# Where a product's two operands begin in SBUF: other strips between the pools of a decoder trunk

## The chip, the cores and the metric

The kernel runs on one core of one Trainium2 chip. The metric is the device time of one execution in microseconds (us); lower is better. One core's SBUF has 128 partitions, and "where a tile begins" means the byte of each partition at which it begins.

## The reference

The reference is a decoder trunk of two layers on 512 tokens of width 1024, in fp32. Each layer applies four blocks to x, and after each one adds the result to a scaled x and normalises:

```python
x = layer_norm(a * x + 0.5 * swiglu_ffn(x, w_in[i, 0], w_out[i, 0]))
x = layer_norm(a * x + h)      # layer 0: diff_attention(x); layer 1: pool_mixer(x)
x = layer_norm(a * x + memory_cross_attention(x, mem, wq[i], wkv[i], wo[i]))
x = layer_norm(a * x + 0.5 * swiglu_ffn(x, w_in[i, 1], w_out[i, 1]))
```

`swiglu_ffn` is `(silu(x @ w_gate) * (x @ w_up)) @ w_out` with an inner width of 2816. `diff_attention` has 8 heads with a rotary position code and the difference of two softmaxes. `pool_mixer` takes causal means over windows of 2, 4, 8 and 16 tokens and a small product for each group of columns. The cross attention has 4 heads and 256 memory tokens.

## The kernel before

Stages follow one another: for each layer `ffn_first` (L1362), `mixer` (L1377), `cross_attention` (L1288), `ffn_second` (L1373). Each opens two groups of tile pools: `stage_pools` (L163) holds the weights, raw from the DMA (`ra`, `rc`, `raw`) and split (`wh`, `wl`); `phase_pool` (L149) holds the activations. Pools are laid out one after the other in the order in which they are opened, so that an unused strip between two of them (`pad`, L134) moves the begin of all tiles behind it. `to_x` opens a strip of 448 bytes, `to_w` one of 64 (the constants `APART` = 64, `ROUND` = 512).

**Products.** An fp32 operand is split into a high part and a rest (`split`: ScalarE copies the high part at L114, VectorE subtracts at L115). `mm3` (L193) makes a product of three matmuls, high by high, high by rest and rest by high:

```python
mm(out, w[0], x[0], ...)    # L197: stationary w, moving x
mm(out, w[0], x[1], ...)    # L198
mm(out, w[1], x[0], ...)    # L199
```

The operand named first in the profile (`x<-xh,wh`) is the moving one, streamed through TensorE; the second is the stationary one, 128 x 128, loaded into the array by a weight load (PEld) that runs beside the matmul ahead of it. Moving operands have 512 or 256 columns.

**FFN.** `up` (L560) makes seven block products of 256 columns (`x`, `y`, `z`, moving `xh`, `xl` or `xe`, stationary `wh`, `wl`), which are combined into the four blocks of a Strassen-like scheme. `down` (L675) does the same on the way back, with 512 columns: `px`, `py`, `pz`, moving `wh`, `wl`, stationary `ha`, `hb`. The two alternate: mostly a down-product of 12 matmuls, then 48 matmuls of up-products, and so on. The last three blocks of a stage go through `plain_down` (L762), `ps` with 512 columns and stationary `xe`, whose moving operands are `wh`, `wl` for the first half and `hb`, `ha` for others.

**The other stages.** The differential attention has `q` and `k` (512 columns), `v` (256), scores, and `po<-v,a`. The cross attention has `pk`, `pv` (keys and values of the memory, 256 columns), `xq` (512, and 256 in part of layer 1), `xs` (scores, 256) and `xo` (512). `to_tokens` (L437) projects back to the tokens: `ps` with 512 columns, moving `wh`, `wl` and other tiles in which weights were split, stationary `oT`. The pool mixer has band products and `pooled`.

**Order.** `weave` (L202) interleaves a main stream of products with a side stream by counted costs; on each engine the instructions stand in program order. DMAs of weights are issued from SP's queue (L574, L225) and, with an addition, from GpSimd's (L578). A tile in a pool that takes over bytes of an earlier pool waits for the last reader of these bytes; so the order of pools also decides which loads wait for what.

**The start of the pool mixer** (layer 1). While its first products run, `load_memory` (L1156) transposes the memory tokens and splits them into `mem0h`, `mem0l` and on (L1175, L114, L115), the keys `pk` of two heads are made early, and `pool_weights` (L1061) loads `pw` (L1066), `ps` (L1073, the scale; L1074, the bias) and multiplies them on VectorE.

Of the kernel before, what the change touches and what calls it, by code (L numbers as in the profile page):

```python
# [9 lines left out]
F32 = mybir.dt.float32  # L10
# [7 lines left out]
P = 128  # L18
# [33 lines left out]
APART, ROUND, LINE = 64, 512, 480  # L52
# [52 lines left out]
class Trunk:  # L105
# [31 lines left out]
            pool = ctx.enter_context(self.pool("pad"))  # L137
            pool.tile([P, nbytes // 4], F32, tag="pad", name="pad")

    def to_x(self, ctx):  # L140

        self.pad(ctx, ROUND - APART)

    def to_w(self, ctx):

        self.pad(ctx, APART)

    @contextmanager
    def phase_pool(self, gain, spare, **bufs):  # L149

        self.gain, self.spare, self.bufs, self.phase = gain, spare, bufs, {}
        with ExitStack() as ctx:
            for t in bufs:
                if t == "_x":
                    self.to_x(ctx)
                else:
                    self.phase[t] = ctx.enter_context(self.pool(t))
            yield  # L160

    @contextmanager
    def stage_pools(self, w, raw, order):  # L163

        with ExitStack() as ctx:
            self.stage = {}
            for n in order:
                if n == "wl" and order[0] == "mem" or n == "wh" == order[0]:
                    self.to_w(ctx)
                self.stage[n] = ctx.enter_context(self.pool(n))  # L170
            self.banks = {n: ctx.enter_context(self.pool(n, space=PSUM)) for n in ("px", "py", "yz")}
            self.w_bufs, self.raw_bufs, self.aux_turn = w, raw, 0
            yield
# [982 lines left out]
    def load_memory(self, tag=None):  # L1156

        nc = self.nc
        src = self.a["mem"][0].rearrange("(m p) (h d) -> p m h d", p=P, h=2)
        if tag:  # L1160
            raw = [[self.tmp(tag) for h in range(2)] for m in range(2)]
            for m in range(2):
                for h in range(2):
                    nc.sync.dma_start(raw[m][h], src[:, m, h])
        else:
            t = self.raw_tile((2, 2, S))
            nc.sync.dma_start(t, src)
            raw = [[t[:, m, h] for h in range(2)] for m in range(2)]
        self.memT = []
        for c in range(0, KC, 2):  # L1170
            pt = self.aux("pt").rearrange("p (c m n) -> p c m n", c=2, m=2)
            for i in range(2):
                for m in range(2):
                    o = (c + i) % 4 * P
                    self.nc.tensor.transpose(pt[:, i, m], raw[m][c // 4][:, o : o + P], self.ident)  # L1175
            t = tuple(self.stage["mem"].tile([P, 2, MEM], F32R, name=f"mem{c}{n}") for n in "hl")
            self.split(t[0], t[1], pt.rearrange("p c m n -> p c (m n)"))
            self.memT += [(t[0][:, i], t[1][:, i]) for i in range(2)]
        if tag and LINE < 480:
            self.stage["mem"].tile([P, (480 - LINE) // 4], F32, name="mempad")  # L1180

    def xa_kv(self, w, h):
        nc = self.nc
# [102 lines left out]
            yield from self.xa_head(*self.heads[h][1])  # L1286

    def cross_attention(self, layer, ln):  # L1288
        bufs = dict(q=8, oT=10, gb=2)
        if layer == 0:  # L1290
            self.kv = []
            mem = self.side_pool("mem")
            with self.other_pools():
                self.stage["mem"] = mem
                with self.phase_pool(("gb", "gb"), "p", pT=6, p=4, kv=8, _x=0, **bufs):
                    self.kvp = self.phase["kv"]
                    with self.tc.high_priority():
                        self.load_memory("p")
                    self.xa(layer, ln)
            self.close_side()  # L1300
        else:
            with self.later, self.phase_pool(("gb", "gb"), "p", _x=0, pT=6, p=4, **bufs):
                self.xa(layer, ln)

    def xa(self, layer, ln):
# [44 lines left out]
        self.side.pop().__exit__(None, None, None)  # L1350

    def ffn_pools(self):
        return self.stage_pools(4, dict(ra=4, rc=3), ("wh", "wl", "ra", "rc"))

    def other_pools(self, order=("wh", "wl", "raw")):
        return self.stage_pools(5, dict(raw=2), order)

    def ffn_phase(self, **more):
        bufs = dict(b1=1, b3=1, b2=1, b4=1, _x=0, xe=6, hb=4, sp=4, ha=4, sr=1, hr=3)
        return self.phase_pool(("hr", "sr"), "sp", **bufs, **more)  # L1360

    def ffn_first(self, layer, ln):  # L1362
# [13 lines left out]

    def mixer(self, layer, ln):  # L1377
        if layer == 0:
            bufs = dict(low=4, rt=2, a=4, p=4, o=1, qk=8, _x=0, v=4, oT=11)
            with self.other_pools(), self.phase_pool(("v", "v"), "rt", **bufs):  # L1380
                self.diff_attention(layer, ln)
            self.close_side()
        else:
            self.later = ExitStack()
            self.later.enter_context(self.other_pools(("mem", "wl", "raw", "wh")))
            self.kvp = self.later.enter_context(self.pool("kv"))
            bufs = dict(pw=1, pb=2, ps=2, ones=1, _x=0, pooled=20, sq=1)
            with self.phase_pool(("pooled", "pooled"), "sq", **bufs):
                side = self.pool_mixer(layer, ln)
                with self.tc.high_priority():  # L1390
                    self.load_memory()
                next(side)
                self.kv = []
                self.weave(self.early_kv(layer, 2), side, 900, 4300)
            self.close_side()
# [45 lines left out]
```

## Time and profile before

| | |
|---|---|
| time, median of 3 runs | 1972.75 us (1970.02 to 1975.78) |
| the profiled execution | 1976.36 us |
| its span in the trace | 1974.6 us |
| granted TensorE clock | 0.995 |
| DMA | 277.96 MB, mean 141 GB/s |
| GpSimd busy | 320.1 us (16%) |

The span is the time from the first to the last recorded instruction of the profiled execution. Rows of the timeline give the start in us, the length in us, the engine, the line of the kernel, the operation, and out<-in; a bracket at the end gives the idle time before and what ended it. The length of a matmul in the profile holds the depth of the pipeline: consecutive matmuls overlap, and how fast they follow is read from the starts.

### The profile page before, as it was taken

How to read it: one execution, taken by the hardware profiler on the slowest of the kernel's cores; microseconds unless marked ns; L12 is line 12 of the kernel's file. 1: busy time of each engine (PE TensorE's matmuls, PEld its weight loads, DVE VectorE, ACT ScalarE, POOL GpSimd, SP SyncE). 2: the span in 40 equal slices, each digit the busy share in tenths (PEclk: the TensorE clock that was granted, in tenths of full speed). 3: DMA queues.
4: the chain of work that ended last, by engine and by line, in shares of the span. 5: the costliest groups of instructions: out<-in, count | busy, mean ns of one | idle time of the engine just before them, and what ended most of it. 6: DMA issues, size and time to landing. Idle time of an engine off the chain costs nothing. (4 is left out here: it accounts for less than half of the span.)

```text
span 1974.6 us, 32506 instructions
## 1 busy us (share of the span) xinstructions
PE 1920.2 (97%) x13104; PEld 1749.0 (89%) x13104; DVE 1566.1 (79%) x2208; ACT 1016.0 (51%) x1545; POOL 320.1 (16%) x297
## 2 busy tenths in 40 slices
PE   7999999999999999999999999999999999999998
PEld 7999998888778888999998999999788889899996
DVE  7888987888867558789887888888777457888886
ACT  5554553466655435555553655555445435555552
POOL 1122121111211002221220311211100013111211
PEclk9999999999999999999999999999989999999999
DMA  9988772322134316977783787877254336877861
GB/s 238 197 171 181 166 156 64 89 65 86 45 116 139 108 65 160 203 176 166 145 193 112 149 176 168 181 171 139 77 171 131 104 96 143 168 173 170 184 143 46
DMA packets 246743, 277.96 MB, mean 141 GB/s; under 512 B 8256, under 2 KB 212544, under 8 KB 246592
## 3 DMA queue, kind: packets, MB, share of 16 engines
q0 software_dynamic: 92928, 92.29, 30.3%
q1 hardware_dynamic: 153664, 183.59, 28.8%
q8 instruction: 103, 1.69, 0.3%
q14 instruction: 48, 0.39, 0.1%
HBM read 273.75 MB, written 2.10 MB: 140 GB/s over the span
## 5 line engine op out<-in xcount | busy, mean ns | idle before, releaser
L578 POOL DMA_DIRECT2D ra<-in_ffn_w_in_dram x132 | 171.4, 1316 | 1017.0 <-DVE wl L115 850.9
L114 ACT CAST wh<-ra 128x1024 fp32r<-128x1024 f32 x184 | 192.9, 1053 | 218.1 <-DMA ra<-in_ffn_w_in_dram 55.7
L115 DVE TENSOR_TENSOR wl<-ra,wh 128x1024 fp32r<-128x1024 f32 x184 | 223.6, 1221 | 82.1 <-ACT wh L114 81.4
L114 ACT CAST wh<-rc 128x1024 fp32r<-128x1024 f32 x136 | 142.7, 1053 | 129.3 <-PE x L198 39.2
L197 PE MATMUL x<-xh,wh 128*128 128x256 f32 x704 | 197.5, 281 | 6.3 <-DVE hr L644 4.1
L197 PE MATMUL x<-xe,wh 128*128 128x256 f32 x704 | 195.3, 277 | 3.1 <-ACT sp L639 1.7
L198 PE MATMUL x<-xl,wh 128*128 128x256 f32 x704 | 196.5, 279 | 1.5 <-DVE xl L115 1.5
L199 PE MATMUL x<-xh,wl 128*128 128x256 f32 x704 | 196.1, 279 | 0.8 <-DVE wl L115 0.8
L198 PE MATMUL x<-xe,wh 128*128 128x256 f32 x704 | 194.8, 277 | 0.0
L199 PE MATMUL x<-xe,wl 128*128 128x256 f32 x704 | 194.7, 277 | 0.0
L115 DVE TENSOR_TENSOR wl<-rc,wh 128x1024 fp32r<-128x1024 f32 x136 | 164.6, 1220 | 27.5 <-ACT wh L114 27.1
L114 ACT CAST wh<-b 128x1024 fp32r<-128x1024 f32 x112 | 117.7, 1051 | 125.7 <-PE x L198 62.0
L115 DVE TENSOR_TENSOR wl<-b,wh 128x1024 fp32r<-128x1024 f32 x112 | 136.8, 1222 | 41.0 <-ACT wh L114 41.0
L197 PEld LDWEIGHTS x<-xh,wh 128*128 128x128 f32 x704 | 133.2, 189 | 9.4 <-issue 4.4
L197 PEld LDWEIGHTS x<-xe,wh 128*128 128x128 f32 x704 | 132.2, 188 | 5.0 <-ACT ha L639 1.9
L198 PEld LDWEIGHTS x<-xl,wh 128*128 128x128 f32 x704 | 133.4, 189 | 3.3 <-DVE xl L115 2.1
L199 PEld LDWEIGHTS x<-xh,wl 128*128 128x128 f32 x704 | 133.2, 189 | 1.0 <-DVE wl L115 1.0
L198 PEld LDWEIGHTS x<-xe,wh 128*128 128x128 f32 x704 | 132.3, 188 | 1.3
L199 PEld LDWEIGHTS x<-xe,wl 128*128 128x128 f32 x704 | 132.4, 188 | 0.0
L115 DVE TENSOR_TENSOR wl<-raw,wh 128x1024 fp32r<-128x1024 f32 x64 | 80.5, 1264 | 56.1 <-ACT wh L114 55.4
L114 ACT CAST wh<-raw 128x1024 fp32r<-128x1024 f32 x64 | 66.6, 1051 | 71.5 <-PE xq L198 22.7
L199 PE MATMUL z<-xh,wl 128*128 128x256 f32 x352 | 97.9, 280 | 4.0 <-DVE wl L115 4.0
(413 smaller groups left out, 6156.5 us busy)
## 6 DMA issues: line engine op xcount, KB each, us to landing
ra<-in_ffn_w_in_dram POOLq DMA_DIRECT2D x132, 512.0 KB, 7.2
rc<-in_ffn_w_in_dram SPq DMA_DIRECT2D x88, 512.0 KB, 6.0
b<-in_ffn_w_out_dram SPq DMA_DIRECT2D x76, 512.0 KB, 5.7
ra<-in_ffn_w_in_dram SPq DMA_DIRECT2D x44, 512.0 KB, 4.7
rc<-in_ffn_w_in_dram POOLq DMA_DIRECT2D x44, 512.0 KB, 9.8
raw<-in_xa_wkv_dram SPq DMA_DIRECT2D x16, 1024.0 KB, 5.3
raw<-in_da_w_qkv_dram SPq DMA_DIRECT2D x16, 512.0 KB, 5.2
raw<-in_xa_wq_dram SPq DMA_DIRECT2D x8, 1024.0 KB, 5.1
```

Of the source, the lines that this page charges most:

```text
L114: self.nc.scalar.copy(hi, src),
L115: self.nc.vector.tensor_sub(lo, src, hi.bitcast(F32)),
L197: mm(out, w[0], x[0], start=start, stop=False, skip_group_check=again)
L198: mm(out, w[0], x[1], start=False, stop=False, skip_group_check=again)
L199: self.last_mm = mm(out, w[1], x[0], start=False, stop=stop, skip_group_check=again)
L578: nc.gpsimd.dma_start(t, source(*block), accum_op=ALU.add)
```

## The change

The rule by which strips are put between pools becomes explicit. A name that begins with `_` in a list of pools is now a strip: `_off` one of 64 bytes, any other (`_on`, `_on_gb`) one of 448. The strips stand at other places than before.

```diff
-    def to_x(self, ctx):
-        self.pad(ctx, ROUND - APART)
-    def to_w(self, ctx):
-        self.pad(ctx, APART)
+    def step(self, ctx, name):
+        self.pad(ctx, APART if name == "_off" else ROUND - APART)
...
             for t in bufs:
-                if t == "_x":
-                    self.to_x(ctx)
+                if t[0] == "_":
+                    self.step(ctx, t)
...
             for n in order:
-                if n == "wl" and order[0] == "mem" or n == "wh" == order[0]:
-                    self.to_w(ctx)
-                self.stage[n] = ctx.enter_context(self.pool(n))
+                if n[0] == "_":
+                    self.step(ctx, n)
+                else:
+                    self.stage[n] = ctx.enter_context(self.pool(n))
...
-        if tag and LINE < 480:
-            self.stage["mem"].tile([P, (480 - LINE) // 4], F32, name="mempad")
+        if tag:
+            self.stage["mem"].tile([P, (ROUND - APART) // 4], F32, name="strip")
...
-        bufs = dict(q=8, oT=10, gb=2)
+        bufs = dict(_off=0, q=8, _on=0, oT=10, _on_gb=0, gb=2)
...
-                with self.phase_pool(("gb", "gb"), "p", pT=6, p=4, kv=8, _x=0, **bufs):
+                with self.phase_pool(("gb", "gb"), "p", pT=6, p=4, kv=8, **bufs):
...
-            with self.later, self.phase_pool(("gb", "gb"), "p", _x=0, pT=6, p=4, **bufs):
+            with self.later, self.phase_pool(("gb", "gb"), "p", pT=6, p=4, **bufs):
...
-        return self.stage_pools(4, dict(ra=4, rc=3), ("wh", "wl", "ra", "rc"))
+        return self.stage_pools(4, dict(ra=4, rc=3), ("_off", "wh", "wl", "ra", "rc"))
...
-        bufs = dict(b1=1, b3=1, b2=1, b4=1, _x=0, xe=6, hb=4, sp=4, ha=4, sr=1, hr=3)
+        bufs = dict(b1=1, b3=1, b2=1, b4=1, _on=0, xe=6, _off=0, hb=4, sp=4, ha=4, sr=1, hr=3)
...
-            bufs = dict(low=4, rt=2, a=4, p=4, o=1, qk=8, _x=0, v=4, oT=11)
+            bufs = dict(low=4, rt=2, a=4, p=4, o=1, qk=8, v=4, oT=11)
...
-            self.later.enter_context(self.other_pools(("mem", "wl", "raw", "wh")))
+            self.later.enter_context(self.other_pools(("_off", "mem", "_on", "wl", "raw", "wh")))
...
-            bufs = dict(pw=1, pb=2, ps=2, ones=1, _x=0, pooled=20, sq=1)
+            bufs = dict(pw=1, pb=2, ps=2, ones=1, _off=0, pooled=20, sq=1)
```

(`other_pools` without a list kept its order; there `to_w` stood ahead of `wh`, and in layer 1's mixer ahead of `wl`. Now the first has no strip.) The computation is the same, and so is the number of instructions on every engine.

What this does to the operands can be worked out from the order and the sizes of the pools: the first byte of the moving operand less that of the stationary operand, modulo 512, which the text calls the distance or the class.

| products | columns | matmuls | distance before | distance after |
|---|---|---|---|---|
| `x`, `y`, `z` (up) | 256 | 6336 | 448 | 448 |
| `px`, `py`, `pz` (down) | 512 | 1344 | 64 | 0 |
| `ps<-wh,xe` and `wl` (plain down) | 512 | 288 | 64 | 64 |
| `ps<-hb,xe`, `ps<-ha,xe` (plain down) | 512 | 288 | 0 | 64 |
| `q`, `k` | 512 | 384 | 448 | 0 |
| `v` | 256 | 384 | 64 | 0 |
| `po<-v,a` | 256, 128 | 160 | 448 | 0 |
| `ps<-wh,oT`, `qk`, `low`, `p`, `kv` (to tokens) | 512 | 480 | 64 | 0 |
| `ps<-q,oT` (to tokens) | 512 | 96 | 0 | 64 |
| `xq` | 512 | 336 | 448 | 0 |
| `xq` | 256 | 96 | 448 | 0 |
| `xo` | 512 | 96 | half 0, half 448 | 0 |
| `pk` | 256 | 384 | 448 | 64 |
| `pv`, `xs` | 256 | 576 | 64 | 448 |
| `pooled` | 256 | 96 | 64 | 448 |

Where pools lie otherwise, some tiles take over the bytes of other tiles than before. The order of instructions is the same on every engine, but for the start of the pool mixer in layer 1: there the loads of the scale and the bias stand on SP ahead of that of `pw`, and VectorE's product of the two ahead of the split that makes `mem2l`.

## The prediction

> **What bounds the kernel now.** I read the page first: the busy table for the engine that binds, then the chain.
>
> ```profile
> span 1974.6 us, 32506 instructions
> ...
> PE 1920.2 (97%) x13104; PEld 1749.0 (89%) x13104; DVE 1566.1 (79%) x2208; ACT 1016.0 (51%) x1545; POOL 320.1 (16%) x297
> ...
> PE 11%; DVE 3%; DMA 2%; issue 0%; ACT 0%; POOL 0%; DVEq 0%; POOLq 0%; ACTq 0%
> ```
>
> TensorE is busy 1920.2 of 1974.6 us, so at most 54.4 us of the span are its idle time. The chain of waits is a weak witness (its shares add up to 16%), but PE leads it. The waits of PE come next (its sum, its times, its longest, in us):
>
> ```profile
> PE pt L434 <- DMA X<-in_x_dram: 5.2, 1, 5.2
> PE x L197 <- DVE hr L644: 4.1, 4, 1.4
> PE z L199 <- DVE wl L115: 4.0, 2, 3.4
> ```
>
> The largest wait is the first load; the others are short and at the seams between stages. So what a product takes on PE sets the end, and the change acts there. The profile's length of one product (0.39 us with 512 columns, below) has the pipeline's depth in it; the price is the distance from start to start, read from the timeline of PE (start, length, then the instruction). Ahead of each product stands its **distance class**: where the moving operand begins less where the stationary one does, modulo 512 bytes of a partition, from the table of the change.
>
> A cycle of the FFN, class 64 in the 512-column down-product, class 448 in the 256-column up-products:
>
> ```profile
> 112.50 0.39 PE L197 MATMUL pz<-wh,hb 128*128 128x512 f32 x1
> ...
> 115.25 0.28 PE L197 MATMUL x<-xe,wh 128*128 128x256 f32 x1
> ...
> 115.84 0.28 PE L199 MATMUL x<-xe,wl 128*128 128x256 f32 x1
> ...
> 120.72 0.39 PE L197 MATMUL px<-wh,hb 128*128 128x512 f32 x1
> ```
>
> 12 down-products from 112.50 to 115.25 are 229.2 ns each; the next 5 up-products take 0.59 us, 118 ns each; the 43 after them 4.88 us, 113.5 ns each. Five times 4.5 ns, some 23 ns, is a tail that each down-product leaves. Sixty products make 8.22 us.
>
> Class 0 with 512 columns (36 products of the plain down-product):
>
> ```profile
> 1404.25 0.39 PE L197 MATMUL ps<-hb,xe 128*128 128x512 f32 x1
> ...
> 1412.41 0.40 PE L197 MATMUL ps<-wh,xe 128*128 128x512 f32 x1
> ```
>
> 8.16 us / 36 = 226.7 ns, two of the 113.3 ns at which 256-column products run at their best (`pv` in term 5). One kind of product with 512 columns, `xo`, is in class 0 in layer 0 (here entered from class 448) and in class 448 in layer 1:
>
> ```profile
> 710.38 0.40 PE L197 MATMUL xo<-pT,kv 128*128 128x512 f32 x1
> ...
> 711.08 0.39 PE L197 MATMUL xo<-pT,kv 128*128 128x512 f32 x1
> ...
> 711.76 0.39 PE L197 MATMUL xq<-xh,wh 128*128 128x512 f32 x1
> ...
> 1555.10 0.39 PE L197 MATMUL xo<-pT,kv 128*128 128x512 f32 x1
> ...
> 1557.90 0.28 PE L197 MATMUL xs<-kv,q 128*128 128x256 f32 x1
> ```
>
> The six in layer 0 take 1.38 us, 230 ns each: the first three 233, the last three 226.7. The twelve in layer 1 take 2.80 us, 233.3 each. So products fall into a steady beat after some slow ones, and the beat depends on the class. The Trainium skill, "TensorE: Matmul & The Clock Gate", Step-by-step, says that PE reads the streaming operand and the next weights by two independent ports, so that loading the next weights takes no bandwidth from the running matmul; by it these distances should make no difference. The trace of before speaks against that (233.3 beside 226.7 ns).
>
> **The change, term by term.** The order of PE's 13104 products is the same, so each term is a number of products by a difference of beats, all on PE's path.
>
> 1. FFN down-products, 64 to 0: 1344 in 112 groups of 12. The likely beat is 226.7 ns, since a group is entered from 113.3 ns products that are in step with it: 12 x (229.2 - 226.7) = 30 ns a group, 3.3 us. Whether the 23 ns tail goes (2.6 us in all) no row shows; I take half, 1.3 us. **-4.6 us**, from 0 to -5.9, and a loss is the rival below.
> 2. `q`, `k`, `xq` and half of `xo`, 448 to 0: 384 + 336 + 48 = 768 products. Ends: 226.7 ns (the long run) and 233.3 (nothing gained). They come in runs of 12 to 24, broken by attention work, so part of each is the slow entry; the nearest row is `xo` in six, 230, and runs of 12 and more have more products after the entry; I take 229.2, 4.1 ns: **-3.2 us**, from 0 to -5.1.
> 3. Products that project to tokens, 64 to 0: 480, in runs of 12 to 24. The old beat is 229.2, the new 226.7 to 230: **-0.5 us**, from -1.2 to +0.4.
> 4. The plain down-products' halves `hb` and `ha` (288) and `ps<-q,oT` (96) go the other way, 0 to 64: up to 2.5 ns each, +1.0 us; part are in the slow entry now, so **+0.6**, from 0 to +1.0.
> 5. 256 columns outside the FFN. The rows: `pk` (448), `pv` (64), `v` (64):
>
> ```profile
> 629.14 0.28 PE L197 MATMUL pk<-mem0h,wh 128*128 128x256 f32 x1
> ...
> 634.48 0.28 PE L199 MATMUL pk<-mem6h,wl 128*128 128x256 f32 x1
> ...
> 635.95 0.28 PE L197 MATMUL pv<-wh,mem0h 128*128 128x256 f32 x1
> ...
> 638.67 0.28 PE L197 MATMUL xs<-kv,q 128*128 128x256 f32 x1
> ...
> 348.95 0.28 PE L197 MATMUL v<-wh,xh 128*128 128x256 f32 x1
> ...
> 354.49 0.28 PE L199 MATMUL v<-wh,xl 128*128 128x256 f32 x1
> ```
>
> 47 `pk` take 113.6 ns, 24 `pv` 113.3, 47 `v` 117.9: class 64 runs in either of two beats, 448 in the good one here. `pk` (384) goes to 64: 0 to +1.7, taken +0.6. `pv` and `xs` (576) go to 448: 0 to -2.6, taken -0.8. `v` (384) goes to 0, a class whose beat with 256 columns no long run shows: 0 to -1.7, taken -0.4. `pooled` and the 256-column `xq` (192): -0.4 to +0.4, taken -0.2. Together **-0.8**, from -4.7 to +2.1.
> 6. The pool mixer's start. The pools of layer 1 lie otherwise, and two DMAs (`pool_scale`, `pool_b`) leave ahead of `pool_w` on SP, not behind it; then DVE's multiply of `ps` stands ahead of `mem2l`, for which PE waits now:
>
> ```profile
> 1431.27 0.37 SPq L1066 DMA_DIRECT2D pw<-in_pool_w_dram  x1
> ...
> 1433.67 0.52 SPq L1073 DMA_DIRECT2D ps<-in_pool_scale_dram  x1
> ...
> 1434.65 0.68 DVE L115 TENSOR_TENSOR mem2l<-pt,mem2h 128x512 fp32r<-128x512 f32 x1
> ...
> 1435.39 0.39 PE L198 MATMUL pk<-mem2l,wh 128*128 128x256 f32 x1 [1.16 <-DVE mem2l L115]
> ```
>
> If the two loads have landed, the multiply (half of 128x1024 words, as `mem2l` is: 0.68 us) stands in DVE's queue for that long, part of it in its idle time; if they are late, `mem2l`, queued behind, and PE wait with it. **+0.5**, from 0 to +1.5.
> 7. Two loads on SP now wait for a split that frees their bytes, and the loads issued behind them wait too:
>
> ```profile
> 303.12 0.41 SPq L225 DMA_DIRECT2D raw<-in_da_w_qkv_dram  x1
> ...
> 311.40 1.22 DVE L115 TENSOR_TENSOR wl<-ra,wh 128x1024 fp32r<-128x1024 f32 x1
> ...
> 341.71 1.05 ACT L114 CAST wh<-raw 128x1024 fp32r<-128x1024 f32 x1
> ...
> 1601.42 0.50 SPq L574 DMA_DIRECT2D ra<-in_ffn_w_in_dram  x1
> ...
> 1606.26 0.37 SPq L574 DMA_DIRECT2D rc<-in_ffn_w_in_dram  x1
> ...
> 1610.87 0.69 DVE L115 TENSOR_TENSOR kv<-raw,kv 128x512 fp32r<-128x512 f32 x1 [0.61 <-ACT kv L114]
> ...
> 1619.30 1.22 DVE L115 TENSOR_TENSOR wl<-ra,wh 128x1024 fp32r<-128x1024 f32 x1
> ```
>
> ```profile
> ra<-in_ffn_w_in_dram SPq DMA_DIRECT2D x44, 512.0 KB, 4.7
> ```
>
> The first `da_w_qkv` load leaves when the split of 311.40 ends, at 312.6 and not 303.1, still 29 us ahead of its use at 341.71; the plain down-product hides it. The `ra` load of 1601.42 leaves when the split of `kv` ends, at 1611.6, with `rc` behind it, and lands some 5 us later (4.7, the median of its queue on the page), ahead of the DVE split at 1619.30 that reads it. There too the plain down-product is the cover; without it PE would stand for up to 2 us. **+0.3**, from 0 to +2.
>
> Sum: -4.6 - 3.2 - 0.5 + 0.6 - 0.8 + 0.5 + 0.3 = **-7.7 us**. The profiled execution took 1976.36 us (span 1974.6 and 1.8 around it), so it would take 1968.7; the median of the runs shown is 3.6 lower, 1972.75, which gives **1965.0 us**. Of that nothing is late next in the FFN: the DVE that splits weights is 79% busy and PE's waits for `wl` are a few us in all, so 0.6% more speed doesn't reach them.
>
> **The rivals.**
>
> *Slower: the products after a class 0 group fall into the bad beat.* The up-products also have two beats. The only way from class 0 into class 448 that the trace shows is this one:
>
> ```profile
> 1099.13 0.28 PE L197 MATMUL x<-xh,wh 128*128 128x256 f32 x1
> ...
> 1101.84 0.28 PE L199 MATMUL x<-xh,wl 128*128 128x256 f32 x1
> ...
> 1178.88 0.28 PE L197 MATMUL z<-xh,wh 128*128 128x256 f32 x1
> ...
> 1187.30 0.28 PE L197 MATMUL z<-xe,wh 128*128 128x256 f32 x1
> ```
>
> 23 up-products at 2.71 / 23 = 117.8 ns, up to a transpose; and the bad beat can last: a cycle of 60 at 1178.88 takes 8.42 us where 8.22 is usual. If every group led to it, 112 x (0.20 + 0.04) = 27 us would be added to the forecast: 1992. It is slower than before by 0.3% (5.9 us) from (7.7 + 5.9) / 0.24, 57 of 112 groups, on; 1979 there. For it: the row above. Against it: the last product of that group stood at distance 448 from the weights of the next, while after the change it stands at 0; and 226.7 is two beats of 113.3, so a group would hand over in step.
>
> *Nothing happens: the class isn't the cause.* Then the beats come with the kinds of product, and terms 6 and 7 are left: 1973.6. The Trainium skill's sentence above is this rival's rule. Against it: `xo`, one kind, has 233.3 throughout in the one class and settles at 226.7 in the other. A milder form is that each short run spends itself in its slow entry, which leaves some 3 of the 7.7 us: 1970.
>
> *More than forecast: every product reaches its good beat at once.* Terms at their far ends, -5.9 - 5.1 - 1.2 - 4.7 + 0.8 = -16.1: 1957.
>
> **How the numbers follow.** The forecast, 1961 to 1969, has 0.47; nothing or little, 1969 to 1976, 0.28; the bad beat, 1976 to 1992, 0.20; more, below 1961, 0.05. A measurement of this kernel tells about 0.3% from no change, 1966.8 to 1978.7. Of the forecast some 0.36 lies below 1966.8, with the 0.05 that is 0.41 faster; the rest of the forecast, the little and a part of the bad beat, 0.42, is the same; 0.17 is slower. The range for 8 in 10 goes from 1959 to 1980: it leaves out 0.04 below, and the bad beat in more than half of the groups, 0.15, above.
>
> **What would show it.** In the changed kernel's timeline of PE: down groups of 12 in 2.72 us (not 2.75), the following up-products at 113.3 at once (term 1) or at 117.8 to the next group (the rival); cycles of 8.17, 8.22 or 8.42 us. Layer 1's twelve `xo` in 2.75 us or less, not 2.80 (term 2). `ps<-hb,xe` at 229 (term 4). PE's wait for `mem2l` longer or gone (term 6); a new wait for `wl` at 1620 to 1630 (term 7). The prediction is wrong if class 0 groups keep a mean of 229 or more, or if the up-products after them are slower than now.

## The result, and the profile after

The changed kernel takes 1984.08 us (median of 6 runs, 1981.94 to 1985.64) and the kernel before 1973.11 us (6 runs): a ratio of 1.0054, with a 95% interval of 1.0041 to 1.0067. It is 11.0 us slower. I had forecast 1965.0 us and a range that ended at 1980.

The profiled execution took 1985.64 us, 9.3 more than that of before. The head of its page:

```profile
span 1983.9 us, 32502 instructions
...
PE 1931.2 (97%) x13104; PEld 1766.2 (89%) x13104; DVE 1565.5 (79%) x2208; ACT 1014.6 (51%) x1545; POOL 321.5 (16%) x297
```

PE has the same 13104 products and is busy 11.0 us longer, and the span is 9.3 us longer, so the loss is in what a product takes. The granted clock, 0.995 and 0.994 in the two executions, explains little of it. The timeline of PE, the same cycle of the FFN as the one quoted from before (the lines of the changed kernel are four earlier, so L193 is what L197 was):

```profile
113.72 0.39 PE L193 MATMUL pz<-wh,hb 128*128 128x512 f32 x1
...
116.44 0.28 PE L193 MATMUL x<-xe,wh 128*128 128x256 f32 x1
...
122.10 0.39 PE L193 MATMUL px<-wh,hb 128*128 128x512 f32 x1
```

(The two traces hold 7392 up-products, seven products of 24 matmuls for each of 44 blocks, not the 6336 in the table of the change; no sum used that number.) The 12 down-products take 2.72 us, 226.7 each, as forecast. The 48 up-products take 5.66 us, 117.9 ns each, and stay so to the next down group, where they settled at 113.5 before. The cycle of 60 takes 8.38 us and not 8.22. Of 108 rows of up-products behind a down-product, 97 are at 117.8 ns, 8 were before; in each of the 11 at 113.3 the starts show a break of 0.1 to 0.9 us at the seam or just behind it. One of these stands behind the first matmul of a down group, whose other eleven come later; the 26 `y` products just ahead of that matmul, at the same distance, are at 117.7 ns:

```profile
153.00 0.40 PE L193 MATMUL py<-wh,ha 128*128 128x512 f32 x1
153.32 0.39 PE L195 MATMUL y<-xh,wl 128*128 128x256 f32 x1
153.54 0.28 PE L193 MATMUL y<-xh,wh 128*128 128x256 f32 x1
...
155.93 0.39 PE L194 MATMUL py<-wl,ha 128*128 128x512 f32 x1
...
158.44 0.28 PE L193 MATMUL z<-xh,wh 128*128 128x256 f32 x1
...
164.09 0.39 PE L193 MATMUL pz<-wh,hb 128*128 128x512 f32 x1
```

From 153.54 on, 21 products take 2.39 us, 113.8 ns each. The eleven down-products behind them are entered from the fast beat, without a wait; their first three take 231, 233 and 231 ns, the others 226.7, and the 48 up-products from 158.44 on are back at 117.7. So it is in all eight places of this kind: at distance 0 a group leads to the slow beat even where it is entered from the fast one. Before, at distance 64, the same eight groups handed the fast beat on. Summed over the starts of the FFN products that follow without a wait in both profiles, the up-products lost 18.5 us and the down-products gained 3.0.

Outside the FFN the same view shows `k`, `v` and `pk` (class 0, 0 and 64):

```profile
376.40 0.39 PE L193 MATMUL k<-xh,wh 128*128 128x512 f32 x1
...
381.84 0.39 PE L193 MATMUL q<-xh,wh 128*128 128x512 f32 x1
```

```profile
353.29 0.28 PE L193 MATMUL v<-wh,xh 128*128 128x256 f32 x1
...
358.93 0.28 PE L195 MATMUL v<-wh,xl 128*128 128x256 f32 x1
...
664.04 0.28 PE L193 MATMUL pk<-mem0h,wh 128*128 128x256 f32 x1
...
669.57 0.28 PE L195 MATMUL pk<-mem6h,wl 128*128 128x256 f32 x1
```

24 `k` take 226.7 ns each (5.44 us), like other runs that follow without a wait; behind a wait a run of 6 or 9 is entered slowly, at some 231. 47 `v` take 120.0 ns each, slower than either beat of before, and 47 `pk` 117.7.

One stage looks faster in this pair of profiles: from the first `pk` of the pool mixer to its last band product the changed kernel takes 27.2 us, and 33.0 before. The stretch (length, PE busy, count, granted clock, DMA share, GB/s) before, after, and in the run `e2_ffn_alone` (next section), whose pool mixer is that of before:

```profile
1431.08:1464.08 33.00, 28.50 (x184) 0.79 0.61 197
1442.10:1469.30 27.20, 24.57 (x185) 0.87 0.58 178
1441.79:1468.84 27.05, 23.63 (x184) 0.94 0.62 194
```

The run with the mixer of before is as fast as the changed kernel, so the 5.8 us are no effect of the change. Behind waits of 0.5 to 1.5 us the granted clock stood at 0.50 for some time, and that time was longest in the profile of before (0.21 x 33.0 = 6.9 us lost, 3.5 after, 1.6 in the third). What the change does here is small: PE's wait for `mem2l`, before and then after, is

```profile
PE pk L198 <- DVE mem2l L115: 1.2, 1, 1.2
```

```profile
PE pk L194 <- DVE mem2l L115: 1.4, 1, 1.4
```

### The profile page after: what moved, and what is told of

Its sections match the earlier page's. It is cut to its first block, busy times and chain, and to the rows that moved or that the text cites. A ratio compares the mean times of both kernels' runs of the same rounds, so it can differ in the third digit from the quotient of the medians.

```text
span 1983.9 us, 32502 instructions
## 1 busy us (share of the span) xinstructions
PE 1931.2 (97%) x13104; PEld 1766.2 (89%) x13104; DVE 1565.5 (79%) x2208; ACT 1014.6 (51%) x1545; POOL 321.5 (16%) x297
## 5 line engine op out<-in xcount | busy, mean ns | idle before, releaser
L193 PE MATMUL x<-xh,wh 128*128 128x256 f32 x704 | 198.4, 282 | 6.2 <-DVE hr L640 3.5
L193 PE MATMUL x<-xe,wh 128*128 128x256 f32 x704 | 197.4, 280 | 1.8 <-ACT sp L635 1.4
L194 PE MATMUL x<-xe,wh 128*128 128x256 f32 x704 | 197.2, 280 | 0.0
L114 ACT CAST wh<-b 128x1024 fp32r<-128x1024 f32 x112 | 117.8, 1052 | 134.2 <-PE x L194 66.2
L193 PEld LDWEIGHTS x<-xh,wh 128*128 128x128 f32 x704 | 132.3, 188 | 9.1 <-issue 3.8
L193 PEld LDWEIGHTS x<-xe,wh 128*128 128x128 f32 x704 | 132.3, 188 | 3.5 <-ACT sp L635 1.6
```

The source lines that it names most:

```text
L114: self.nc.scalar.copy(hi, src),
L193: mm(out, w[0], x[0], start=start, stop=False, skip_group_check=again)
L194: mm(out, w[0], x[1], start=False, stop=False, skip_group_check=again)
```

## The experiments

**Theory:** up-products of 256 columns have two steady beats, 113.3 and 117.8 ns, and fall into one of them by the moment, within a short period, at which the product ahead of them ends; a down group in class 0 ends at a moment that leads into the slow one. **Rival 1:** the loss is outside the FFN. **Rival 2:** the moved bytes of `hb` themselves slow what runs beside the up-products.

### The FFN's strips undone, and alone

In the changed kernel:

```diff
-        bufs = dict(b1=1, b3=1, b2=1, b4=1, _on=0, xe=6, _off=0, hb=4, sp=4, ha=4, sr=1, hr=3)
+        bufs = dict(b1=1, b3=1, b2=1, b4=1, _on=0, xe=6, hb=4, sp=4, ha=4, sr=1, hr=3)
```

> The changed kernel with the FFN's strips as before (hb again where it began, so that the down-products are at distance 64; all else as changed). Theory of the beat: the 256-column up-products of the FFN take 117.8 ns in the changed kernel because the down-product at distance 0 ends in a step from which they fall into the slow beat. Then FFN cycles of 60 products go back from 8.38 to 8.22 us, the time falls by 108 x 0.14 = 15 us, to about 1969, below before by what the other parts are worth. Rival, the other parts: the loss lies in the products outside the FFN (v at 119.9, pk at 117.8 ns), and undoing the FFN gives back 5 us at most: 1979 or more.

In the kernel before, the strip alone:

```diff
+                elif t == "_off":
+                    self.to_w(ctx)
...
-        bufs = dict(b1=1, b3=1, b2=1, b4=1, _x=0, xe=6, hb=4, sp=4, ha=4, sr=1, hr=3)
+        bufs = dict(b1=1, b3=1, b2=1, b4=1, _x=0, xe=6, _off=0, hb=4, sp=4, ha=4, sr=1, hr=3)
```

> The kernel before with one strip of 64 bytes ahead of hb in the FFN, nothing else. Theory of the beat: cycles of 8.38 us instead of 8.22, down groups at 226.7 ns, up-products at 117.8: 1973 + 15 = 1988. Rival, the other parts: 1973 to 1978.

Undone: 1970.79 us (before on the same chip 1974.95), a ratio of 0.9983 (0.9970 to 0.9997). Alone: 1986.53, a ratio of 1.0057 (1.0034 to 1.0080). The timeline of PE, first undone, then alone:

```profile
180.04 0.39 PE L193 MATMUL px<-wh,hb 128*128 128x512 f32 x1
...
182.78 0.28 PE L193 MATMUL x<-xe,wh 128*128 128x256 f32 x1
...
188.25 0.39 PE L193 MATMUL px<-wh,hb 128*128 128x512 f32 x1
```

```profile
113.35 0.39 PE L199 MATMUL pz<-wh,hb 128*128 128x512 f32 x1
...
116.07 0.28 PE L199 MATMUL x<-xe,wh 128*128 128x256 f32 x1
...
121.73 0.39 PE L199 MATMUL px<-wh,hb 128*128 128x512 f32 x1
```

Undone, the group takes 2.74 us and the 48 up-products 5.47 (114.0); alone, 2.72 and 5.66 (117.9), as in the changed kernel. One strip of 64 bytes makes the loss; rival 1 falls. What is left of the change without it is worth -0.17%, 3.4 us, with an interval from 0.6 to 5.9. At distance 64 both beats keep themselves: in the profile of the kernel with the strips undone, 14 of the 108 rows are at 117.8 ns, seven in a row from 99 us on and seven from 852 on, and before it was 8; a group that is entered from the slow beat leads back to it, until a break in the starts ends the series.

### The seam cut, addresses as they are

```diff
+        mm(out[:, :n], w[0], x[1][:, :n], start=False, stop=False, skip_group_check=True)
+        mm(out[:, n:], w[0], x[1][:, n:], start=False, stop=False, skip_group_check=True)
```

in the place of the last but one matmul of each down group, with n = 256, 384, 448 and 320 in the four stages.

> The changed kernel with all addresses as they are; only the last but one matmul of each down group of 12 is cut into two of fewer columns: 256 and 256 in the first FFN, 384 and 128 in the second, 448 and 64 in the third, 320 and 192 in the fourth. Theory of the beat: the step in which a group ends moves, by another amount in each stage, so in at least one of the four stages the up-products run at 113.3 ns, and the stages differ. Rival, the addresses: with the strip ahead of hb something that reads or writes at the moved bytes slows the up-products; then they stay at 117.8 ns in all four stages.

1976.04 us, one execution. The timeline of PE, from the first up-product of a run of 48 to the next down-product, one run of each stage:

```profile
173.46 0.28 PE L200 MATMUL x<-xe,wh 128*128 128x256 f32 x1
...
178.93 0.39 PE L200 MATMUL px<-wh,hb 128*128 128x512 f32 x1
...
923.53 0.28 PE L200 MATMUL x<-xe,wh 128*128 128x256 f32 x1
...
928.97 0.39 PE L200 MATMUL px<-wh,hb 128*128 128x512 f32 x1
...
1262.30 0.28 PE L200 MATMUL x<-xe,wh 128*128 128x256 f32 x1
...
1267.74 0.39 PE L200 MATMUL px<-wh,hb 128*128 128x512 f32 x1
...
1797.53 0.28 PE L200 MATMUL x<-xe,wh 128*128 128x256 f32 x1
...
1803.18 0.39 PE L200 MATMUL px<-wh,hb 128*128 128x512 f32 x1
```

5.47, 5.44, 5.44 and 5.65 us: fast in three stages, slow in the fourth, at the same addresses. Rival 2 falls. The third has not even a tail (113.3 ns each). But the cut costs what it gains: with the group the cycle takes 8.21 to 8.27 us in the fast stages, because each group is now entered from the fast beat and its first three products take 232 ns, and the cut itself takes 10 to 90 ns.

### The end of the group moved in steps of two columns

```diff
+                if b == k == 1:
+                    n = S - 2 * (self.groups % 16)
...
+        mm(out[:, :n], w[0], x[1][:, :n], start=False, stop=False, skip_group_check=True)
```

> The changed kernel; of the last but one matmul of every FFN down group the last 2 x (g mod 16) columns are left out (g counts the groups, 112 in all), so part of the down-product is not computed and a group ends up to 12.5 ns (30 columns) earlier, in steps of 0.83 ns, with all addresses as they are. Theory of the beat: whether the following up-products run at 113.3 or 117.8 ns is decided by where in a period of 6.67 ns (16 columns) the group ends; so the beat changes with g mod 16, and the same g mod 16 gives the same beat, in all four stages; some 4 to 12 of the 16 are fast. Rival, any break of the even run of matmuls is enough: all groups with columns left out are fast, only g mod 16 = 0 is slow. Rival, the addresses: all are slow.

1986.26 us, one execution. By the starts, the last matmul of a group comes 227 ns after the shortened one at g mod 16 = 0 and 215 ns at 15: 12 ns for 30 columns, some 0.8 ns for two. The timeline of PE, from first up-product to next down-product, for g mod 16 = 6, 11, 12, 0, 1 and 2:

```profile
141.43 0.28 PE L199 MATMUL x<-xh,wh 128*128 128x256 f32 x1
...
146.89 0.39 PE L199 MATMUL px<-wh,ha 128*128 128x512 f32 x1
...
183.26 0.28 PE L199 MATMUL x<-xe,wh 128*128 128x256 f32 x1
...
188.92 0.39 PE L199 MATMUL px<-wh,hb 128*128 128x512 f32 x1
...
191.63 0.28 PE L199 MATMUL x<-xh,wh 128*128 128x256 f32 x1
...
197.07 0.39 PE L199 MATMUL px<-wh,hb 128*128 128x512 f32 x1
...
225.08 0.28 PE L199 MATMUL z<-xe,wh 128*128 128x256 f32 x1
...
230.74 0.39 PE L199 MATMUL pz<-wh,hb 128*128 128x512 f32 x1
...
233.46 0.28 PE L199 MATMUL x<-xe,wh 128*128 128x256 f32 x1
...
238.90 0.39 PE L199 MATMUL px<-wh,hb 128*128 128x512 f32 x1
...
241.64 0.28 PE L199 MATMUL x<-xe,wh 128*128 128x256 f32 x1
...
247.29 0.40 PE L199 MATMUL px<-wh,hb 128*128 128x512 f32 x1
```

5.46, 5.66, 5.44, 5.66, 5.44 and 5.65 us. Where no wait breaks the run or the one ahead of the group, every group with g mod 16 = 1, 6, 7, 9, 12 or 13 is fast and every other one slow, in all four stages. Two columns less (g mod 16 = 1) are enough, four are too many. (Two groups, one at g mod 16 = 1 and one at 9, stand behind a run that a wait broke, are entered from the fast beat and not from the slow one, and lead to the slow beat.) So it isn't that any break heals it, and it isn't chance: with all addresses as they are, the moment of the hand-over sets the beat. The period of 16 columns was put in by the experiment; shifts beyond it were not tried, so that there is such a period is not shown by this run. Nor does any run show what in the engine keeps the two beats.

### Other distances

The four stages of the changed kernel with other strips (bytes ahead of `wh` and ahead of `hb`; one execution each):

```diff
+STRIPS = {(0, 0): (64, 32), (0, 1): (64, 96), (1, 0): (0, 0), (1, 1): (448, 448)}
...
+STRIPS = {(0, 0): (64, 384), (0, 1): (64, 320), (1, 0): (64, 192), (1, 1): (64, 128)}
```

> The changed kernel with other strips in each FFN stage. Distances of the down-products and the up-products: 32 and 448 in the first, 480 and 448 in the second, 0 and 0 in the third, 0 and 64 in the fourth. Theory of the beat: which beat the up-products fall into depends on both distances; 512 columns at 32 or 480 need not run at 226.7 ns, and the stages differ from one another. If 226.7 ns in the down group always brings the slow beat, stages three and four stay at 117.8 or slower. Rival, the addresses of hb alone: the stages with hb moved by other than 0 bytes (all but the third) all have up-products at 117.8 ns, the third at 113.3.

> The changed kernel with the down-products of the four FFN stages at distances 192, 256, 384 and 448 and the up-products at 448 as they are. Theory of the beat: each distance has a beat of its own for 512 columns (448: 233.3, as xo showed) and hands over to the fast or the slow beat of the up-products, the same in all groups of a stage. If the distance of 0 is special (both operands begin alike), none of these has 226.7 ns. Rival, the rule depends on the distance modulo 64 only: all four stages look like the changed kernel, 226.7 and 117.8.

And a strip between `wh` and `wl`:

```diff
-("_off", "wh", "wl", "ra", "rc")
+("_off", "wh", "_w", "wl", "ra", "rc")
```

> The changed kernel with one more strip, between wh and wl, in the FFN stages: 64, 192, 128 and 256 bytes in the first to the fourth. The first and third matmul of each down-product stay at distance 0, the second goes to 64, 192, 128 and 256; in the up-products the third goes to 384, 256, 320 and 192, the others stay at 448. Theory of the beat: since the runs with the down-products at 256 looked like those at 0, distances count modulo 256, and the fourth stage looks like the changed kernel (226.7 and 117.8 ns); in the others the down group is slower than 226.7 and its end, and with it the beat of the up-products, is another one, which I can't say beforehand. Rival, distances count modulo 512: the fourth stage differs as the others do.

They took 1994.29, 1981.90 and 1985.40 us. From the timelines, the usual run of 48 up-products in each stage (medians of the starts; where a row has two values, cycles of the one and of the other kind follow each other in turn):

| down | up | ns per down-product | ns per up-product | cycle, us |
|---|---|---|---|---|
| 64 (before, and undone) | 448 | 229.0 | 113.9 | 8.21 |
| 0 (changed) | 448 | 226.7 | 117.8 | 8.37 |
| 32 | 448 | 233.2 | 117.8 | 8.45 |
| 480 | 448 | 232.8 | 113.6 | 8.25 |
| 0 | 0 | 228.9 | 119.9 | 8.50 |
| 0 | 64 | 229.7 | 117.9 | 8.41 |
| 256 | 448 | 226.7 | 117.8 | 8.37 |
| 192 or 448 | 448 | 233.3, 232.4 | 113.8, 117.9 | 8.26, 8.45 |
| 384 | 448 | 231.3, 231.2 | 113.5, 117.8 | 8.23, 8.43 |
| 0, with the second at 64 | 448, the third 384 | 231.0 | 118.1 | 8.44 |
| 0, with the second at 192 | 448, the third 256 | 232.0 | 117.8 | 8.44 |
| 0, with the second at 128 | 448, the third 320 | 232.3 | 114.4 | 8.28 |
| 0, with the second at 256 | 448, the third 192 | 226.7 | 117.8 | 8.37 |

256 looks like 0, alone and as a step between `wh` and `wl`, and 448 looks like 192: these distances count modulo 256, not 512, and not 64. At 192, 384 and 448 a group that is entered from the fast beat leads to the slow one, and the next one back. So what a group hands on depends on its distance and on the beat in which it is entered: 64 keeps either, these three turn it, and 0 and 256 were seen to lead to the slow one alone. My rival for the first of the three (`hb`'s bytes) had its third stage fast; it is the slowest of all. No pair of distances here has 226.7 and 113.3 together, and the best cycle is that of before.

### The rest of the change

`v` moved to 448 and `pk` to 448, `q` and `k` to 64, the FFN undone:

```diff
-            self.stage["mem"].tile([P, (ROUND - APART) // 4], F32, name="strip")
+            self.stage["mem"].tile([P, APART // 4], F32, name="strip")
...
-            with self.other_pools(), self.phase_pool(("v", "v"), "rt", **bufs):
+            with self.other_pools(("_on", "wh", "wl", "raw")), self.phase_pool(("v", "v"), "rt", **bufs):
...
-            self.later.enter_context(self.other_pools(("_off", "mem", "_on", "wl", "raw", "wh")))
+            self.later.enter_context(self.other_pools(("_on", "mem", "_off", "wl", "raw", "wh")))
```

> The FFN's strips as before, the other products by the beats that the runs so far showed: v at distance 448 (113.3 ns expected; 119.9 at 0, 117.8 at 64) and with it q and k at 64 (229, not 226.7), pk at 448 (113.4, not 117.8), pv at 64 (113.4 after pk), xq, xo and the products to tokens at 0 as changed. Theory of the beat: against the version with only the FFN undone (1970.8) v gains 384 x 6.5 = 2.5 us, q and k lose 384 x 2.3 = 0.9, pk gains 384 x 4.4 = 1.7, pv loses up to 0.2: 3 us, 1967.7, 0.35% below before. Rival, the hand-over: v after q and k at 64, and pv at 64, fall into the slow beat; then nothing is gained, 1970 to 1972.

1982.54 us, a ratio of 1.0050 (1.0032 to 1.0068): a miss. The timeline of PE and its waits:

```profile
640.93 0.28 PE L193 MATMUL pk<-mem0h,wh 128*128 128x256 f32 x1
...
646.47 0.28 PE L195 MATMUL pk<-mem6h,wl 128*128 128x256 f32 x1
```

```profile
PE pt L1171 <- DMA p<-in_mem_dram: 10.5, 2, 10.3
```

The hand-over again: 47 `pk` at 448 behind `xq` at 0 take 117.9 ns each, where the same products at the same distance, behind `xq` at 448, took 113.6 before. Over the starts, against the version with the FFN undone, `pk` gained 0.4 of the 1.7 us that I expected, and `v` 1.0 of 2.5. And a wait of 10.3 us is new; the next two runs settle what it is. With the FFN and layer 0's mixer as before:

```diff
-            bufs = dict(low=4, rt=2, a=4, p=4, o=1, qk=8, v=4, oT=11)
-            with self.other_pools(), self.phase_pool(("v", "v"), "rt", **bufs):
+            bufs = dict(low=4, rt=2, a=4, p=4, o=1, qk=8, _on=0, v=4, oT=11)
+            with self.other_pools(("_off", "wh", "wl", "raw")), self.phase_pool(("v", "v"), "rt", **bufs):
```

> The changed kernel with the FFN's strips and those of layer 0's mixer as before (down-products at 64, q and k at 448, v at 64, po at 448, its products to tokens at 64), the cross attention and the pool mixer as changed. Theory of the beat: in the profiles the changed mixer takes 2.6 us longer (v at 119.9 ns and the products with 128 and 256 columns lose more than q and k gain), so 1970.8 less 2.6, 1968.2, 0.3% below before. Rival, the beats add up as I priced them (q and k gain 2.5 us, v loses nothing): undoing the mixer costs 2 us, 1973.

1983.20 us, 1.0052 (1.0039 to 1.0066), a miss again: the mixer was about 1.5 us faster on the way than with only the FFN undone, and then came the same wait. SP's loads of the memory tokens and the ScalarE instructions ahead of them, in the timeline:

```profile
607.11 1.15 ACT L370 ACTIVATE rt<-X,mean 128x1024 bf16<-128x1024 f32 x1 [2.16 <-DVE mean L357]
608.17 0.19 ACT L370 ACTIVATION_READ_ACCUMULATOR rt<-X,mean 128x1 f32 x1
608.38 0.80 SPq L1160 DMA_DIRECT2D p<-in_mem_dram  x2
```

Then `p` moved by the same 64 bytes:

```diff
-                with self.phase_pool(("gb", "gb"), "p", pT=6, p=4, kv=8, **bufs):
+                with self.phase_pool(("gb", "gb"), "p", _off_p=0, pT=6, p=4, kv=8, _off=0, q=8, _384=0, oT=10, _on_gb=0, gb=2):
```

> The version with the FFN's strips and those of layer 0's mixer as before took 1983 us and not 1968: PE stood 10 us at the start of the first cross attention, because the loads of the memory tokens into p were issued at 608 us, after the last instruction of ScalarE that writes rt, and not at 575. Theory: with 64 bytes more ahead of the mixer's pools, p (which did not move) lies over the end of rt. This kernel moves p, and what follows it, by the same 64 bytes (384 instead of 448 bytes further on, so that oT stays). Then the loads leave at about 575 again, the stall is gone, and the time is 1968 to 1970, faster than before. Rival: the stall comes from the order of the loads on SP, whatever lies where; then it stays, 1980 to 1984.

1972.34 us (above the 1968 to 1970 expected), a ratio of 0.9986 (0.9975 to 0.9997), and in the timeline of SP

```profile
574.57 2.69 SPq L1160 DMA_DIRECT2D p<-in_mem_dram  x4
```

The loads leave 34 us earlier and the wait is gone: `p` had begun 64 bytes ahead of the end of `rt`, which ScalarE still wrote at 608 us. (In the run with `v` and `pk` moved, whose mixer had a strip of 448 bytes, it began 448 bytes ahead of that end.) This version and the one with the FFN alone undone (0.9983) are both a little faster than the kernel before; the intervals overlap, so which of the two is better is open.

## Why the prediction was wrong

**What bounds the kernel.** Right: PE's products set the end, and the loss came from their beats.

**Term 1, the step that failed.** The first half held: 226.7 ns, 2.72 us a group, and 3.0 us in the profiles for the 3.3 forecast. The second half, the hand-over to the up-products, failed: I had put -1.3 us for it, half of the tail, and thought a slow hand-over unlikely, since a group would be entered from 113.3 ns products "in step" with it and 226.7 is two beats of 113.3. The up-products cost 18.5 us more in the profiles. That one beat is twice the other does not say that they meet at the same moment. In the changed kernel the even 226.7 follows on the slow beat, and leads back to it (226, 227, 227 at once); entered from the fast one, at 155.93 above and in the cut, it starts with three products of some 232, so it isn't in step, and at 155.93 it led to the slow beat all the same. The group ends at a moment, and the scan shows that two columns less already give the other beat. I had forecast -4.6 us for the term; with the strip alone the kernel lost 0.57%.

**The slower rival was the case.** It named the mechanism, the place and the row of before that showed it (1099.13). I gave it 0.20, arguing that there the last product had been at distance 448 from the next weights and would be at 0 after the change; the slow beat came all the same. Its price was a little too high: it put 0.24 us a group on the forecast's cycle (8.22 less 0.04) and took all 112 groups, 1992; the runs gave 0.20 us (8.38 for 8.18) in 97 rows where 8 had been slow before, and a break in the starts resets the beat in the others.

**Terms 2 to 5.** Together I forecast -3.9 us. Over the starts of the products that follow without a wait in both profiles, term 2 came to -3.2 (forecast -3.2; 4.2 ns each, with the slow entry as I took it), term 3 to -0.45 (-0.5) and term 4 to +0.25 (+0.6). Term 5 came to +2.2, where I had -0.8 and +2.1 at the far end: `v` at 0 went to 120.0 ns, outside both of my ends, the 256-column `xq` at 0 cost 0.6 us, and `pk`, behind `xq` at 0, went into the slow beat (117.7), the far end of its bound. So the four terms came to some -1.1. That the run without the FFN's strip gained 3.4, near my sum, doesn't bear that sum out: its interval, 0.6 to 5.9, holds both.

**Term 6.** Forecast +0.5. The pool mixer took 27.2 us and 27.1 in the run with the mixer of before, and PE's wait for `mem2l` grew by 0.2 us, so the size was about right. Most of the 5.8 us between the two profiles is the half clock's.

**Term 7.** Right as far as the profile shows: no new wait of PE at 341 or at 1620 to 1630. But two of my own kernels met the kind of wait that it looked for, 10 us of it.

**No effect, and more than forecast.** The first is refuted by the FFN's strip alone: the same 13104 products took 11 us longer on PE when operands began elsewhere. The rule that I named behind this rival, that loading the next weights takes no bandwidth from the running matmul (the Trainium skill, "TensorE: Matmul & The Clock Gate", Step-by-step), therefore does not predict these times; whether the load of weights is what takes them, no run shows. The second, that every product reaches its good beat at once, is refuted by the up-products at 117.8 ns.

## What to carry to other kernels

The time of a product at its steady best does not say what it does to the products behind it. Measure a change of layout over a whole cycle, with the seam in it, and look at starts, not lengths: two steady beats of the same product show up only there. Before a gain in one stage is put down to the change, look at a run in which that stage is as it was: here 5.8 us of it came without the change. And whoever moves a pool should look for what its tiles now lie over: 64 bytes cost 10 us.

## What the hardware did that I had not expected

- The same 256-column product, with the same operands, runs steadily at 113.3 or at 117.8 ns, for as long as nothing interrupts it, and two columns at the seam (some 0.8 ns by the starts) decide.
- Distances of 0 and 256 bytes behave alike (226.7 and 117.8 ns); 256 columns at distance 0 take 120 ns.
- Behind waits of 0.5 to 1.5 us PE ran at a granted clock of 0.50 for 3 to 14 us, an estimate from the mean clock of the windows above (0.94, 0.87 and 0.79). Products of 256 columns took some 213 ns there. It was longer in one execution than in another of the same stage: two profiles differed by 6 us there without any cause in the change.
